# A two-layer transformer trunk on one core: the MLP's first eight blocks by halves of the tokens, and output products without the last pair of heads placed earlier

## The chip, the cores and the metric

One core of one Trainium2 chip runs the whole program. The metric is the device time of one launch in microseconds. A core has TensorE (PE, with its weight loads PEld), VectorE (DVE), ScalarE (ACT), GpSimd (POOL), and SyncE (SP), which issues the DMAs. A number like L238 is a line of the kernel.

## The reference

Two layers over 512 tokens (S) of width 1024 (D). Eight heads are dilated windowed attention, eight are latent attention with low-rank queries and keys.

```python
for l in range(DEPTH):                               # DEPTH = 2
    mod = c_act @ w_mod[l] + b_mod[l]
    sh1, sc1, gt1, sh2, sc2, gt2 = jnp.split(mod, 6, axis=-1)
    h = rms_norm(x, g_norm_mix[l]) * (1.0 + sc1[:, None]) + sh1[:, None]
    proj = h @ w_in[l]
    q_d, k_d, v_d, cq, ckv, k_rope = jnp.split(proj, cuts, axis=-1)
    ...
    o_dil = dilated_attention(q_d, k_d, v_d, positions, slopes)
    o_mla = latent_attention(cq, ckv, k_rope, positions, ...)
    mix = jnp.concatenate([o_dil, o_mla], axis=-1) @ w_out[l]
    x = x + gt1[:, None] * mix
    h = rms_norm(x, g_norm_mlp[l]) * (1.0 + sc2[:, None]) + sh2[:, None]
    y = jnp.square(jax.nn.relu(h @ w_mlp_in[l])) @ w_mlp_out[l]
    x = x + gt2[:, None] * y
```

## The kernel before

Activations lie transposed: x is eight tiles `xT[j]` of 128 features by 512 tokens. Each float32 operand is kept as a high and a low part, and each product is three matmuls into one PSUM bank (`mm3`): high by high (L238), low weight by high (L239), high weight by low (L240). Weights are split as they arrive (`load_split`): SP issues the DMA into a "raw" tile, ACT copies the high part (L233), POOL subtracts it for the low part (L234).

Tiles come from pools by tag, each with a fixed number of buffers. "wh" and "wl" hold split weights, "pt" transposed probabilities, "qk" queries and keys, "ot" outputs of heads, "zz" scratch; in PSUM there are four banks "mm", two "sc" and two "tr". A tile waits until the former user of its buffer is done. A scheduler orders the instructions of each engine when the kernel is built, from the order in which the program issues them; each engine then works through its own list in order.

A layer has these stages.
- Norm and first projection. `norm` works on one half of the tokens: squares and sums (L255 to L259), one matmul for the sum over features (L284), the inverse root on DVE and ACT (L285 to L290), then eight chunks. Even chunks take an "sc" bank (DVE L273, ACT L274, DVE L275), odd ones a "b" tile (DVE L268, ACT L269, POOL L270, L271). High and low parts come out as `h`. In layer 1 the weights of projection 0 (`PR[0]`, 384 columns, four blocks of 128 tokens `tb`) and of the latent projection (`W`, 416 columns) follow each other.
- Heads, two at a time: `heads` yields the steps of a pair, and `weave` puts other work between them at fixed points (the table of numbers; "W1", "OL0" and so on are entries of it). A head ends in ACT L370, DVE L371. The pair then is split: ACT L651 (high), POOL L652 (low), into an "ot" tile. The dilated heads' half of the output projection (`out_dil`) runs during the latent heads.
- The latent heads' half of the output projection. Features j = 0 to 7, each four products k = 0 to 3, where k = 3 is the last pair of heads, for half of the tokens at a time; `add_x` (DVE L659) adds the result to x. In half 0 three features are in flight: products 0 to 2 of j + 1 and j + 2 are issued before product 3 of j.
- The MLP. The first group has eight blocks of 128 features. Blocks 0 to 3 are done for half 0 of the tokens, then for half 1 (24 matmuls of 256 each), blocks 4 to 7 for all tokens (24 matmuls of 512). After each block come the squared relu and its split (ACT L832, DVE L833, ACT L834, DVE L835). Then follow the second MLP product of this group and the other groups. In layer 0, `next_mod` computes the modulation of layer 1 on the side: a DMA into a tile, and DVE L170; two go with each of blocks 4 to 7.

Of the kernel before, what the change touches and what calls it, by code (L numbers as in the profile page):

```python
# [34 lines left out]
    F0=(0, 0), F1=(6.4, 2.33), T0=(3.23, 2.08), T1=(8.8, 8.8), M0=(0, 0), M1=(4, 4), M2=(4.1, 4.1),  # L35
    M3=(6.5, 6.55), LD0=(5, 5), LD1=(9, 9), LM=(6.45, 7.11), LO=(7.2, 7.2), OD0=(3.1, 3.1), OD1=(5.1, 5.1),
    OL0=(3.5, 3.5), OL1=(10.04, 10.04), MV0=(1.5,), MV1=(3.75,), MV2=(5.37,), MV3=(8,), MV4=(0.62,),
    MV5=(6.55,), MP0=(3.45,), MP1=(8.6,), W0=(13.54,), W1=(21.5,), W2=(33,),
)


# [1 line left out]
def trunk(ctx: ExitStack, tc: tile.TileContext, a):  # L43
# [20 lines left out]
    def t4(tag, shape, dt=F32R):  # L64
        return pool.tile(list(shape), dt, tag=tag, bufs=BUFS[tag], name=nm(tag))
# [7 lines left out]
    def ps(tag, shape=(128, 512)):  # L73
        return psum.tile(list(shape), F32, tag=tag, bufs=BUFS[tag], name=nm(tag))
# [138 lines left out]
    def next_mod(**kw):  # L213
        if modq:
            modq.pop(0)(**kw)
# [10 lines left out]
        V.scalar_tensor_tensor(r, t, 1.5, y, op0=OP.add, op1=OP.mult)  # L226
        return r

    def load_split(src, n, raw="raw"):
        raw = t4(raw, [128, 1024], F32)[:, :n]  # L230
        hi, lo = t4("wh", [128, 1024])[:, :n], t4("wl", [128, 1024])[:, :n]
        SY.dma_start(raw, src)
        A.activation(hi, raw, AF.Copy)  # L233
        G.tensor_tensor(lo, raw, f(hi), op=OP.subtract)  # L234
        return hi, lo
# [142 lines left out]
    for l in range(L):  # L378
# [19 lines left out]
        def group(src, n):  # L398
            ws = {}

            def load(i, raw="raw"):
                hi, lo = load_split(src[i], 2 * n, raw)
                ws[i] = (hi.rearrange("p (k n) -> p k n", k=2), lo.rearrange("p (k n) -> p k n", k=2))

            def step(bank, k, tb):
                mm3(bank, hx(hh, k, tb * 128, tb * 128 + 128), hx(hl, k, tb * 128, tb * 128 + 128),
                    ws[k // 2][0][:, k % 2], ws[k // 2][1][:, k % 2], k == 0, k == 7)

            return [lambda i=i, **kw: load(i, **kw) for i in range(4)], step

        def blocks(w, n, step, chain):
            for tb in range(4):
                st = {}

                def mm(k, tb=tb, st=st):
                    if k == 0:
                        st["b"] = ps("mm")
                    step(st["b"][:, :n], k, tb)

                w["mm"].append([lambda k=k, mm=mm: mm(k) for k in range(8)])  # L420
                w["chain"].append(lambda tb=tb, st=st: chain(tb, st["b"]))

        def dil_prep(pr, k_outer=False):
            w = dict(mm=[], chain=[])
            w["load"], step = group(a["win"][l, pr], 384)
            R = {}

            def chain(tb, bank):
                half, t = tb // 2, tb % 2
                if tb == 0:  # L430
                    R["QS"], R["KH"], R["KL"] = (t4("qk", [128, 2, S]) for _ in range(3))
                    R["VD"] = t4("qk", [128, 4, 2, 2, 64])
                if t == 0:
                    R[half] = t4("pt" if k_outer else "zz", [128, 2, 4, 2, 64], F32)

                nb = 2 if l == 0 else 1
                if t == 0 or nb == 1:
                    R["sq"], R["bank"] = s2([128, 4 * nb, 64]), []
                sq, got = R["sq"], R["bank"]
                got.append((t, bank))  # L440
                A.activation(sq[:, 4 * len(got) - 4:4 * len(got)].rearrange("p h d -> p (h d)"), bank[:, 0:256],
                             AF.Square, scale=1.0 / 8)

                def values():
                    src = bank[:, 256:384].rearrange("p (h d) -> p h d", h=2)
                    vt = R["VD"][:, tb]
                    A.activation(vt[:, :, 0], src, AF.Copy)
                    V.tensor_tensor(vt[:, :, 1], src, f(vt[:, :, 0]), op=OP.subtract)

                if nb == 2:  # L450
                    values()
                if len(got) == nb:
                    v = small(4 * nb)
                    V.tensor_reduce(v, sq, axis=AX.X, op=OP.add)
                    rs = rsqrt_tiny(v, 4 * nb, bank)
                    for u, (t_, bk) in enumerate(got):
                        src = bk[:, 0:256].rearrange("p (h o d) -> p h o d", h=4, o=1).to_broadcast([128, 4, 2, 64])
                        scl = rs[:, 4 * u:4 * u + 4].rearrange("p (h o d) -> p h o d", o=1, d=1).to_broadcast([128, 4, 2, 64])
                        V.tensor_tensor(R[half][:, t_], src, scl, op=OP.mult)
                if nb == 1:  # L460
                    values()

            def tail(half):
                dq = R[half]
                for is_k in range(2):
                    tr = ps("mm", (128, 2, 2, 128))
                    for hd in range(2):
                        for t in range(2):
                            T.transpose(tr[:, hd, t], dq[:, t, 2 * is_k + hd].rearrange("p a b -> p (a b)"), ident)  # L469
                    src = tr.rearrange("p h t c -> p h (t c)")  # L470
                    if is_k:
                        kh, kl = R["KH"][:, :, HALF[half]], R["KL"][:, :, HALF[half]]
                        A.activation(kh, src, AF.Copy, scale=kcol)
                        V.scalar_tensor_tensor(kl, src, kcol, f(kh), op0=OP.mult, op1=OP.subtract)
                    else:
                        q = R["QS"][:, :, HALF[half]]
                        A.activation(q, src, AF.Copy)
                        V.tensor_tensor(q[64:128], src[64:128], f(q[64:128]), op=OP.subtract)

            def score(hd, sc, qb):  # L480
                q = R["QS"][:, hd, qb * 128:(qb + 1) * 128]
                T.matmul(sc, q, R["KH"][:, hd], start=True, stop=False)
                T.matmul(sc, q, R["KL"][:, hd], start=False, stop=True)

            w["score"], w["vals"] = score, lambda hd, kc: R["VD"][:, kc, hd].rearrange("p a b -> p (a b)")
            w["tail"] = [lambda half=half: tail(half) for half in range(2)]
            if k_outer:
                w["step"], w["do_chain"] = step, chain
            else:
                blocks(w, 384, step, chain)  # L490
            return w


# [167 lines left out]
        wo = {}  # L661

        def out_load(half, jj):
            hi, lo = load_split(a["wout"][l, half, jj], 1024)
            wo[half, jj] = (hi.rearrange("p (j k m) -> p j k m", j=2, k=4), lo.rearrange("p (j k m) -> p j k m", j=2, k=4))

        def out_dil(j):
# [96 lines left out]
        else:  # L764
            gains()
            for fn in PR[0]["load"]:
                fn()
            run(flow(PR[0], 0, 16) + spread(W["load"], 10, 15.2) + flow(W, 16, 32)
                + [(tn("W0"), PR[0]["tail"][0]), (tn("W1"), PR[0]["tail"][1]), (tn("W2"), W["tail"])])

        for st in range(8):
            ev = []
# [25 lines left out]
            weave(heads(st, PR[st]), ev)  # L798

        h2h, h2l = new_h()  # L800
        for hf in HALF:
            late = []
            for j in range(8):
                wh, wl = wo[1, j // 2]
                p = ps("mm")[:, :256]

                def prod(k, wh=wh, wl=wl, j=j, p=p, hf=hf):
                    mm3(p, wh[:, j % 2, k], wl[:, j % 2, k], OT[4 + k][:, 0, hf], OT[4 + k][:, 1, hf], k == 0, k == 3)

                for k in range(3):  # L810
                    prod(k)

                def finish(prod=prod, j=j, p=p, hf=hf):
                    prod(3)
                    add_x(j, hf, p, gt1)

                late.append(finish)
                if len(late) > (2 if hf.start == 0 and j < 7 else 0):
                    late.pop(0)()
            for fn in late:  # L820
                fn()
            norm(hf, amlp[l], modc[l][:, 24:32], h2h, h2l)


        gt2 = modc[l][:, 40:48]
# [9 lines left out]
            V.tensor_tensor(r2[:, 1, hf], p, f(r2[:, 0, hf]), op=OP.subtract)  # L835

        def w1_tile(i):
            return tuple(t.rearrange("p (k m) -> p k m", k=8) for t in load_split(a["w1"][l, i], 1024))

        R2 = {}  # L840

# [7 lines left out]
        FULL = slice(0, S)  # L849
        for grp in ((0, 8), (8, 16), (16, 24), (24, 28), (28, 32)):  # L850
            rng = range(*grp)
            for i in rng:
                R2[i] = t4(("qk", "ot")[i % 2], [128, 2, S])
            if grp[0] == 0:
                ws = [w1_tile(i) for i in range(4)]
                for hf in HALF:
                    for i in range(4):
                        mlp1(i, hf, ws[i])
                rest = range(4, 8)
            else:  # L860
                rest = rng
            for i in rest:
                mlp1(i, FULL, w1_tile(i))
                if l == 0:
# [91 lines left out]
```

## Time and profile before

| | us |
|---|---|
| median of 3 runs | 1359.0 (1358.58 to 1362.28) |
| profiled execution | 1359.13 |
| its span, first to last instruction | 1357.4 |
| PE busy | 1272.5 |
| mean granted TensorE clock, share of full speed | 0.981 |

The profile lists instructions by line and engine with what ended the idle time before them, as [idle us <-releaser]. The starts of two matmuls in the timeline tell the pace; their listed lengths overlap. In a row of windows the columns are the stretch, its length, the busy time (and number of instructions) of PE, PEld, DVE, ACT and POOL, the granted clock, the DMA's share and GB/s.

### The profile page before, as it was taken

How to read it: one execution, taken by the hardware profiler on the slowest of the kernel's cores; microseconds unless marked ns; L12 is line 12 of the kernel's file. 1: busy time of each engine (PE TensorE's matmuls, PEld its weight loads, DVE VectorE, ACT ScalarE, POOL GpSimd, SP SyncE). 2: the span in 40 equal slices, each digit the busy share in tenths (PEclk: the TensorE clock that was granted, in tenths of full speed). 3: DMA queues.
4: the chain of work that ended last, by engine and by line, in shares of the span. 5: the costliest groups of instructions: out<-in, count | busy, mean ns of one | idle time of the engine just before them, and what ended most of it. 6: DMA issues, size and time to landing. Idle time of an engine off the chain costs nothing.

```text
span 1357.4 us, 19211 instructions
## 1 busy us (share of the span) xinstructions
PE 1272.5 (94%) x6922; PEld 1108.0 (82%) x6922; DVE 752.4 (55%) x1620; ACT 675.5 (50%) x1405; POOL 650.6 (48%) x504
## 2 busy tenths in 40 slices
PE   4878979898899999999998999899889999999999
PEld 2878867787888888888898999798788888888888
DVE  6777797876661661834575577987672122121123
ACT  5567798776541322323245677887654133232321
POOL 5636776671554444444435443444155444444441
PEclk9979998999999999999998999999999999999999
DMA  9325543331254572854532344311013332223221
GB/s 344 111 94 175 177 155 108 104 130 74 63 187 147 189 253 93 280 169 160 170 108 83 90 138 135 94 48 48 1 63 109 96 103 96 93 93 108 95 93 62
DMA packets 57246, 167.59 MB, mean 123 GB/s; under 512 B 8640, under 2 KB 10816, under 8 KB 57152
## 3 DMA queue, kind: packets, MB, share of 16 engines
q1 hardware_dynamic: 57152, 166.38, 37.1%
q8 instruction: 54, 0.88, 0.3%
q14 instruction: 40, 0.33, 0.1%
HBM read 155.87 MB, written 10.49 MB: 123 GB/s over the span
## 4 chain that ended last, share of the span: by engine, by line
PE 72%; DVE 6%; ACT 6%; POOL 4%; issue 4%; DMA 3%; POOLq 0%; ACTq 0%; DVEq 0%
PE mm L238 21%; PE mm L239 21%; PE mm L240 21%; PE tr L368 2%; PE tr L358 2%; POOL wl L234 2%; DMA raw<-in_wout_dram 1%; DVE pt L362 1%; ACT wh L233 1%; DVE P L343 1%; POOL b L339 1%; POOL raw L167 1%; DMA bias<-b 1%; PE sc L238 1%; PE mm L469 1%
## 5 line engine op out<-in xcount | busy, mean ns | idle before, releaser
L234 POOL TENSOR_TENSOR wl<-raw,wh 128x1024 fp32r<-128x1024 f32 (+3 forms) x188 | 425.2, 2266 | 448.9 <-ACT wh L233 426.9
L233 ACT ACTIVATE wh<-raw 128x1024 fp32r<-128x1024 f32 (+3 forms) x188 | 188.8, 1005 | 272.0 <-PE mm L240 206.2
L659 DVE SCALAR_TENSOR_TENSOR x<-mm,mod,x 128x512 f32<-128x512 f32 (+1 forms) x144 | 89.0, 630 | 261.4 <-PE mm L240 261.2
L238 PE MATMUL mm<-h,wh 128*128 128x512 f32 (+1 forms) x608 | 224.5, 370 | 7.1 <-ACT h L274 7.1
L239 PE MATMUL mm<-h,wl 128*128 128x512 f32 (+1 forms) x608 | 224.5, 370 | 0.0
L240 PE MATMUL mm<-h,wh 128*128 128x512 f32 (+1 forms) x608 | 221.8, 369 | 1.1 <-POOL h L271 1.1
L238 PE MATMUL mm<-ot,wh 128*128 128x512 f32 (+1 forms) x448 | 155.9, 350 | 4.5 <-ACT ot L651 4.1
L239 PE MATMUL mm<-ot,wl 128*128 128x512 f32 (+1 forms) x448 | 154.5, 347 | 0.0
L240 PE MATMUL mm<-ot,wh 128*128 128x512 f32 (+1 forms) x448 | 151.4, 348 | 0.2 <-POOL ot L652 0.2
L832 ACT ACTIVATE P<-mm 128x512 f32<-128x512 f32 (+1 forms) x72 | 39.2, 551 | 201.7 <-PE mm L240 201.7
L238 PEld LDWEIGHTS mm<-h,wh 128*128 128x128 f32 x608 | 116.2, 191 | 26.0 <-ACT h L274 7.5
L239 PEld LDWEIGHTS mm<-h,wl 128*128 128x128 f32 x608 | 116.1, 191 | 19.2 <-POOL wl L234 0.2
L240 PEld LDWEIGHTS mm<-h,wh 128*128 128x128 f32 x608 | 114.6, 190 | 20.1 <-POOL h L271 1.5
L833 DVE SCALAR_TENSOR_TENSOR mm<-mm,P 128x512 f32<-128x512 f32 (+1 forms) x72 | 45.4, 636 | 138.9 <-ACT P L832 138.9
L238 PE MATMUL mm<-wh,h 128*128 128x384 f32 (+1 forms) x288 | 98.9, 356 | 15.5 <-ACT h L742 9.8
L239 PE MATMUL mm<-wh,h 128*128 128x384 f32 (+1 forms) x288 | 101.9, 354 | 5.3 <-POOL h L745 3.2
L238 PE MATMUL mm<-qk,wh 128*128 128x512 f32 (+1 forms) x288 | 105.3, 366 | 1.0 <-DVE x L659 1.0
L239 PE MATMUL mm<-qk,wl 128*128 128x512 f32 (+1 forms) x288 | 105.2, 365 | 0.0
L240 PE MATMUL mm<-qk,wh 128*128 128x512 f32 (+1 forms) x288 | 105.2, 365 | 0.0
L355 POOL TENSOR_SCALAR P<-P,hs 128x512 f32<-128x512 f32 x64 | 48.1, 752 | 112.4 <-DVE hs L348 96.7
L240 PE MATMUL mm<-wl,h 128*128 128x384 f32 (+1 forms) x288 | 100.4, 351 | 0.0
L170 DVE SCALAR_TENSOR_TENSOR pt<-pt,cb 128x1024 f32<-128x1024 f32 x56 | 99.1, 1804 | 0.0
(248 smaller groups left out, 2669.0 us busy)
## 6 DMA issues: line engine op xcount, KB each, us to landing
raw<-in_w_dram SPq DMA_DIRECT2D x64, 512.0 KB, 3.3
pt<-in_wmod_dram SPq DMA_DIRECT2D x56, 512.0 KB, 5.0
raw<-in_w2a_dram SPq DMA_DIRECT2D x48, 512.0 KB, 3.5
raw<-in_wmod_dram SPq DMA_DIRECT2D x24, 512.0 KB, 3.6
raw<-in_win_dram SPq DMA_DIRECT2D x30, 384.0 KB, 3.3
bias<-b SPq DMA_DIRECT2D x32, 256.0 KB, 2.0
raw<-in_wout_dram SPq DMA_DIRECT2D x16, 512.0 KB, 3.5
raw<-in_w2b_dram SPq DMA_DIRECT2D x16, 512.0 KB, 3.3
```

The costliest lines, as they stand in the source:

```text
L170: r = V.scalar_tensor_tensor(w, w, 1.0, cb, op0=OP.mult, op1=OP.mult, accum_out=out)
L233: A.activation(hi, raw, AF.Copy)
L234: G.tensor_tensor(lo, raw, f(hi), op=OP.subtract)
L238: T.matmul(out, sh, mh, start=first, stop=False)
L239: T.matmul(out, sl, mh, start=False, stop=False)
L240: T.matmul(out, sh, ml, start=False, stop=last)
L355: G.tensor_scalar(P, P, r_, 0.0, op0=OP.mult, op1=OP.add)
L358: T.transpose(tr[:, kc], P[:, kc * 128:(kc + 1) * 128], ident)
L368: T.matmul(po[:, HALF[qh]], vals(hd, kc), pt[qh][w][:, kc], start=(kc == 0 and w == 0), stop=(kc == 3 and w == 1))
L659: V.scalar_tensor_tensor(xT[j][:, hf], p, gt[:, j:j + 1], xT[j][:, hf], op0=OP.mult, op1=OP.add)
L832: A.activation(r, p, AF.Relu)
L833: V.scalar_tensor_tensor(p, p, 0.0, r, op0=OP.max, op1=OP.mult)
```

## The change

1. `load_split` takes the tags of the buffers for high and low part.
2. MLP, first group: all eight weight tiles are loaded ahead, tiles 0 and 1 into "pt", 2 and 3 into "qk", 4 to 7 into "wh" and "wl", and all eight blocks go by halves. The eight `next_mod` of layer 0 go with half 1.
3. Layer 1's first projections: the latent weights go into "ot" and "pt"; the blocks alternate, `PR[0]` 0 and 1, `W` 0 and 1, then 2 and 3 of each, and `PR[0]` 2 and 3 use "sc" banks. The result of projection 0 lies in "pt" and the second tail comes at 29.5 instead of 21.5 in the table.
4. Output products of the latent half: in half 0, products 0 to 2 of features 4 to 7 are added to x at once, those of features 0 to 3 stay in the four "mm" banks; then product 3 follows for all eight. Weight tile 3 goes into "zz".

```diff
-    MV5=(6.55,), MP0=(3.45,), MP1=(8.6,), W0=(13.54,), W1=(21.5,), W2=(33,),
+    MV5=(6.55,), MP0=(3.45,), MP1=(8.6,), W0=(13.54,), W1=(29.5,), W2=(33,),
...
-    def load_split(src, n, raw="raw"):
+    def load_split(src, n, raw="raw", tags=("wh", "wl")):
...
-                    R[half] = t4("pt" if k_outer else "zz", [128, 2, 4, 2, 64], F32)
+                    R[half] = t4("pt" if pr == 0 else "zz", [128, 2, 4, 2, 64], F32)
...
-                blocks(w, 384, step, chain)
+                blocks(w, 384, step, chain, ("mm", "mm", "sc", "sc") if pr == 0 else ("mm",) * 4)
...
-            hi, lo = load_split(a["wout"][l, half, jj], 1024)
+            hi, lo = load_split(a["wout"][l, half, jj], 1024, tags=("zz", "zz") if half and jj == 3 else ("wh", "wl"))
...
-            run(flow(PR[0], 0, 16) + spread(W["load"], 10, 15.2) + flow(W, 16, 32)
-                + [(tn("W0"), PR[0]["tail"][0]), (tn("W1"), PR[0]["tail"][1]), (tn("W2"), W["tail"])])
+            for i in range(4):
+                W["load"][i](tags=("pt", "pt") if i == 3 else ("ot", "ot"))
+            ev = []
+            for n, (w, tb) in enumerate(((PR[0], 0), (PR[0], 1), (W, 0), (W, 1), (PR[0], 2), (PR[0], 3), (W, 2), (W, 3))):
+                ev += spread(w["mm"][tb], 4 * n, 4 * n + 3.6) + [(4 * n + 3.8, w["chain"][tb])]
+            run(ev + [(tn("W0"), PR[0]["tail"][0]), (tn("W1"), PR[0]["tail"][1]), (tn("W2"), W["tail"])])
...
-        for hf in HALF:
-            late = []
-            for j in range(8):
...
+        def out_lat(j, p, hf, ks, first, last):
+            wh, wl = wo[1, j // 2]
+            for k in ks:
+                mm3(p, wh[:, j % 2, k], wl[:, j % 2, k], OT[4 + k][:, 0, hf], OT[4 + k][:, 1, hf],
+                    first and k == ks[0], last and k == ks[-1])
+        hf, held = HALF[0], {}
+        for j in (4, 5, 6, 7, 0, 1, 2, 3):
+            p = ps("mm")[:, :256]
+            out_lat(j, p, hf, (0, 1, 2), True, j >= 4)
+            if j >= 4:
+                add_x(j, hf, p, gt1)
+            else:
+                held[j] = p
+        for j in range(8):
+            p = held[j] if j < 4 else ps("mm")[:, :256]
+            out_lat(j, p, hf, (3,), j >= 4, True)
+            add_x(j, hf, p, gt1)
+        norm(hf, amlp[l], modc[l][:, 24:32], h2h, h2l)
...
+            tags = ("wh", "wl") if i >= 4 else ("pt", "pt") if i < 2 else ("qk", "qk")
...
+            ws = [w1_tile(i) for i in range(8)] if grp[0] == 0 else []
...
-                ws = [w1_tile(i) for i in range(4)]
                 for hf in HALF:
-                    for i in range(4):
+                    for i in range(8):
                         mlp1(i, hf, ws[i])
-                rest = range(4, 8)
+                        if l == 0 and hf.start and i:
+                            next_mod(tag="pt", pin=True)
+                            if i == 7:
+                                next_mod(tag="pt", pin=True)
+                rest = ()
```

What the scheduler makes of it shows in each engine's list. TensorE at the MLP's first group of layer 0, where half 0 ends and half 1 begins: before, with `h_3876` the first tile of normalized input and `wh_4263` the weights of block 0, the list has the following.

```order
L238 MATMUL mm_4376<-h_3882,wh_4281 128x256
L239 MATMUL mm_4376<-h_3882,wl_4282 128x256
L240 MATMUL mm_4376<-h_3883,wh_4281 128x256
L238 MATMUL mm_4406<-h_3876,wh_4263 128x256
L239 MATMUL mm_4406<-h_3876,wl_4264 128x256
```

That is block 3 of half 0 followed at once by block 0 of half 1. After, at the same place:

```order
L238 MATMUL mm_4408<-h_3882,qk_4281 128x256
L239 MATMUL mm_4408<-h_3882,qk_4282 128x256
L240 MATMUL mm_4408<-h_3883,qk_4281 128x256
L238 MATMUL mm_4438<-h_3876,wh_4287 128x256
L239 MATMUL mm_4438<-h_3876,wl_4288 128x256
```

Block 3 of half 0 is followed by block 4 of half 0 (`wh_4287`); blocks 4 to 7 are 96 matmuls, and the first of half 1 (on `pt_4263`) comes behind them.

POOL at the last pair of heads of layer 0 (`P_` are probabilities, `ot_3867` the last pair's tile, `raw_` weights as loaded), before:

```order
L355 TENSOR_SCALAR P_3811<-P_3811,hs_3810 128x512
L355 TENSOR_SCALAR P_3836<-P_3836,hs_3835 128x512
L652 TENSOR_TENSOR ot_3867<-o_3622,ot_3867 128x512
L234 TENSOR_TENSOR wl_4264<-raw_4262,wh_4263 128x1024
L234 TENSOR_TENSOR wl_4270<-raw_4268,wh_4269 128x1024
```

and after:

```order
L355 TENSOR_SCALAR P_3811<-P_3811,hs_3810 128x512
L234 TENSOR_TENSOR qk_4282<-raw_4280,qk_4281 128x1024
L355 TENSOR_SCALAR P_3836<-P_3836,hs_3835 128x512
L234 TENSOR_TENSOR wl_4288<-raw_4286,wh_4287 128x1024
L234 TENSOR_TENSOR pt_4264<-raw_4262,pt_4263 128x1024
L234 TENSOR_TENSOR pt_4270<-raw_4268,pt_4269 128x1024
L652 TENSOR_TENSOR ot_3867<-o_3622,ot_3867 128x512
```

Four splits of the MLP's weights, of tiles 3, 4, 0 and 1, now stand ahead of the last pair's L652, where they stood behind it or much later.

ACT at the same place, before:

```order
L361 ACTIVATE pt_3744<-tr_3816 128x4x128
L361 ACTIVATE pt_3744<-tr_3841 128x4x128
L370 ACTIVATE o_3622<-tr_3848 64x512
L651 ACTIVATE ot_3867<-o_3622 128x512
L255 ACTIVATE sc_3998<-x_77 128x256
```

and after:

```order
L361 ACTIVATE pt_3744<-tr_3816 128x4x128
L233 ACTIVATE wh_4287<-raw_4286 128x1024
L361 ACTIVATE pt_3744<-tr_3841 128x4x128
L233 ACTIVATE pt_4263<-raw_4262 128x1024
L233 ACTIVATE pt_4269<-raw_4268 128x1024
L370 ACTIVATE o_3622<-tr_3848 64x512
L651 ACTIVATE ot_3867<-o_3622 128x512
```

Three high parts now stand ahead of the last head's L370; the last two write buffers that its own products read (pt).

More of the change, by code (lines that the diff above doesn't have):

```diff
@@ L227, in rsqrt_tiny @@
         return r
-    def load_split(src, n, raw="raw"):
+    def load_split(src, n, raw="raw", tags=("wh", "wl")):
         raw = t4(raw, [128, 1024], F32)[:, :n]
-        hi, lo = t4("wh", [128, 1024])[:, :n], t4("wl", [128, 1024])[:, :n]
+        hi, lo = t4(tags[0], [128, 1024])[:, :n], t4(tags[1], [128, 1024])[:, :n]
         SY.dma_start(raw, src)
@@ L399, in group, with load @@
             ws = {}
-            def load(i, raw="raw"):
-                hi, lo = load_split(src[i], 2 * n, raw)
+            def load(i, raw="raw", tags=("wh", "wl")):
+                hi, lo = load_split(src[i], 2 * n, raw, tags)
                 ws[i] = (hi.rearrange("p (k n) -> p k n", k=2), lo.rearrange("p (k n) -> p k n", k=2))
@@ L409, in group, with blocks @@
             return [lambda i=i, **kw: load(i, **kw) for i in range(4)], step
-        def blocks(w, n, step, chain):
+        def blocks(w, n, step, chain, tags=("mm",) * 4):
             for tb in range(4):
@@ L416, in mm @@
                     if k == 0:
-                        st["b"] = ps("mm")
+                        st["b"] = ps(tags[tb])
                     step(st["b"][:, :n], k, tb)
@@ L800, in trunk @@
         h2h, h2l = new_h()
-        for hf in HALF:
-            late = []
-            for j in range(8):
[L804 to L822, printed above, removed]
+        def out_lat(j, p, hf, ks, first, last):
[16 more added lines that the diff above has]
+        norm(hf, amlp[l], modc[l][:, 24:32], h2h, h2l)
+        hf = HALF[1]
+        for j in range(8):
+            p = ps("mm")[:, :256]
+            out_lat(j, p, hf, (0, 1, 2, 3), True, True)
+            add_x(j, hf, p, gt1)
+        norm(hf, amlp[l], modc[l][:, 24:32], h2h, h2l)
         gt2 = modc[l][:, 40:48]
@@ L837, in w1_tile @@
         def w1_tile(i):
-            return tuple(t.rearrange("p (k m) -> p k m", k=8) for t in load_split(a["w1"][l, i], 1024))
+            tags = ("wh", "wl") if i >= 4 else ("pt", "pt") if i < 2 else ("qk", "qk")
+            return tuple(t.rearrange("p (k m) -> p k m", k=8) for t in load_split(a["w1"][l, i], 1024, tags=tags))
         R2 = {}
@@ L851, in trunk @@
             rng = range(*grp)
+            ws = [w1_tile(i) for i in range(8)] if grp[0] == 0 else []
             for i in rng:
                 R2[i] = t4(("qk", "ot")[i % 2], [128, 2, S])
+            rest = rng
             if grp[0] == 0:
-                ws = [w1_tile(i) for i in range(4)]
                 for hf in HALF:
-                    for i in range(4):
+                    for i in range(8):
                         mlp1(i, hf, ws[i])
-                rest = range(4, 8)
-            else:
-                rest = rng
+                        if l == 0 and hf.start and i:
[3 more added lines that the diff above has]
+                rest = ()
             for i in rest:
```

## The prediction

> **What bounds the kernel now.** I read the page first, then the waits of PE, then the timeline and windows at the waits that the change touches. The page says who the bound is.
>
> ```profile
> PE 1272.5 (94%) x6922; PEld 1108.0 (82%) x6922; DVE 752.4 (55%) x1620; ACT 675.5 (50%) x1405; POOL 650.6 (48%) x504
> PE 72%; DVE 6%; ACT 6%; POOL 4%; issue 4%; DMA 3%; POOLq 0%; ACTq 0%; DVEq 0%
> PE mm L238 <- ACT h L274: 10.8, 3, 3.7
> PE mm L238 <- ACT ot L651: 4.1, 2, 2.1
> ```
>
> TensorE is busy for 1272.5 of 1357.4 us. All it does is needed, so time is to be had only from its idle 85 us, from its half-speed stretches, and from shape (narrow matmuls cost more per column). Two rows of waits are the change's targets: three waits for the first normalized tile (L274), 10.8 us together, and two for the last pair of heads (L651), 4.1 us. The timeline places them, and the windows show what a wait costs beyond itself.
>
> ```profile
> 361.48 0.59 PE L284 MATMUL tr<-P,ones 128*128 128x256 f32 x2
> 367.46 0.47 ACT L274 ACTIVATE h<-sc,mod 128x256 fp32r<-128x256 f32 x1 [1.86 <-DVE sc L273]
> 367.99 0.58 PE L238 MATMUL mm<-h,wh 128*128 128x256 f32 x1 [3.53 <-ACT h L274]
> 1013.03 0.58 PE L238 MATMUL mm<-h,wh 128*128 128x256 f32 x1 [3.53 <-ACT h L274]
> 1013.42 0.42 PE L239 MATMUL mm<-h,wl 128*128 128x256 f32 x1
> 1013.63 0.41 PE L238 MATMUL mm<-h,wh 128*128 128x256 f32 x1
> ...
> 368.00:370.50 2.50, 2.50 (x11) 2.50 (x12) 2.27 (x7) 1.86 (x5) 1.82 (x3) 0.50 0.00 0
> 370.50:372.00 1.50, 1.50 (x11) 1.50 (x11) 1.35 (x4) 1.10 (x3) 1.40 (x3) 0.75 0.06 11
> ...
> 1007.07 0.28 PE L240 MATMUL mm<-h,wh 128*128 128x256 f32 x1
> 1007.19 0.28 PE L238 MATMUL mm<-h,wh 128*128 128x256 f32 x1
> 1060.00:1290.00 230.00, 230.00 (x1017) 190.50 (x1016) 44.10 (x62) 64.71 (x83) 101.42 (x43) 1.00 0.30 99
> ```
>
> Windows run: length, busy time of PE, PEld, DVE, ACT, POOL, then the granted clock. After the 3.53 us wait the clock is 0.50 for 2.5 us and 0.75 on average over the next 1.5, so half speed lasts about 3.25 us; the starts there are 0.213 us apart (1013.42 to 1013.63) instead of 0.12 (1007.07 to 1007.19): some 14 matmuls at 0.093 extra, 1.3 us. The last row prices the full-width form: 1017 matmuls in 230 us, 0.226 each.
>
> **Part 1, the MLP by halves (both layers).** Before, half 0 of the tokens has 4 blocks of 24 matmuls of 256; the sums for half 1 (L284) go through PE at 361.48, the first h of half 1 starts at 367.46, and PE waits from 364.46. After, 8 blocks stand there. In the order, 12 + 96 matmuls come between the last L284 and the first matmul of half 1: 108 x 0.12 = 13.0 us, against the 6.0 + 0.5 us that the chain from L284 to the first h takes (361.48 to 367.93). The wait goes, and with it the half clock: -3.53 - 1.3. The cost: blocks 4 to 7 are cut from 96 matmuls of 512 to 192 of 256: 96 x (2 x 0.12 - 0.226) = +1.3. Net -3.5 per layer, -7.0 for both. What is late next is nothing on this chain: 6.5 us of slack remain, which also covers an L284 that runs a few us later. By the Trainium skill ("TensorE: Matmul & The Clock Gate", section on the back-to-back issue gap) a warm matmul starts every N/2.4 ns + 2.5 ns, an estimate of 109.2 ns at 256 and 215.8 at 512. By that the narrow form would cost 96 x 2.5 ns = 0.24 us per layer instead of 1.3, and the part would bring 2.1 us more; this trace's spacings, 0.12 and 0.226, are longer than both, and I keep them.
>
> Covers in this part. A block's PSUM bank comes back through L832, L833 and L835.
>
> ```profile
> 362.89 0.64 ACT L832 ACTIVATE P<-mm 128x256 f32<-128x256 f32 x2
> 364.29 0.42 DVE L835 TENSOR_TENSOR qk<-mm,qk 128x256 fp32r<-128x256 f32 x1
> L170 DVE SCALAR_TENSOR_TENSOR pt<-pt,cb 128x1024 f32<-128x1024 f32 x56 | 99.1, 1804 | 0.0
> pt<-in_wmod_dram SPq DMA_DIRECT2D x56, 512.0 KB, 5.0
> ```
>
> That takes 1.8 us (362.89 to 364.71); block 4 starts 22 matmuls (2.6 us) after block 0's last, so I cost it at nothing (1 us per layer if ACT is late). In layer 0 all eight steps of the next layer's modulation move into half 1: 8 x 1.8 = 14.4 us of DVE beside 8 blocks' own work, in 192 x 0.12 = 23 us. The tiles that they load into stand in the buffers of weight tiles 0 and 1, free only after blocks 0 and 1 of half 1 (2.9 and 5.8 us in), and a load takes 5.0 us. DVE may stand still for the first of them, with posts of blocks behind it; four banks give PE about three blocks (8.6 us) of cover. Cost zero, up to 4.
>
> **Part 2, output products of the last pair (both layers).** Before, 36 of the 96 matmuls of half 0 run ahead of the last pair's result; after, 72. So 36 x 0.12 = 4.3 us leave the path behind it.
>
> ```profile
> 328.47 0.59 ACT L370 ACTIVATE o<-tr 64x512 f32<-64x512 f32 x1 [1.91 <-PE tr L368]
> 329.81 0.63 ACT L651 ACTIVATE ot<-o 128x512 fp32r<-128x512 f32 x1 [0.75 <-DVE o L371]
> 330.49 0.58 PE L238 MATMUL mm<-ot,wh 128*128 128x256 f32 x1 [2.06 <-ACT ot L651]
> 330.52 1.27 POOL L652 TENSOR_TENSOR ot<-o,ot 128x512 fp32r<-128x512 f32 x1 [5.82 <-ACT ot L651]
> 332.82 0.48 DVE L659 SCALAR_TENSOR_TENSOR x<-mm,mod,x 128x256 f32<-128x256 f32 x1 [3.04 <-PE mm L240]
> 975.49 0.58 PE L238 MATMUL mm<-ot,wh 128*128 128x256 f32 x1 [2.06 <-ACT ot L651]
> ...
> 300.00:331.00 31.00, 24.59 (x156) 19.95 (x155) 21.03 (x41) 22.55 (x48) 9.54 (x10) 0.99 0.21 75
> 331.25:334.00 2.75, 2.75 (x15) 2.52 (x14) 1.18 (x3) 0.60 (x2) 0.54 (x1) 0.55 0.90 347
> 925.00:976.00 51.00, 45.45 (x290) 38.64 (x288) 33.45 (x66) 36.87 (x76) 14.69 (x18) 0.99 0.06 22
> ...
> L234 POOL TENSOR_TENSOR wl<-raw,wh 128x1024 fp32r<-128x1024 f32 x144 | 344.3, 2394 | 386.2 <-ACT wh L233 381.3 <-PE mm L240 2.7 <-PE mm L239 1.5
> L233 ACT ACTIVATE wh<-raw 128x1024 fp32r<-128x1024 f32 x144 | 152.3, 1057 | 257.6 <-PE mm L240 202.2 <-issue 46.0 <-DMA raw<-in_wout_dram 5.6
> ```
>
> They cost nothing only where PE was idle. PE's idle time before the last pair is 6.4 us in layer 0 (31.00 - 24.59) and 5.5 in layer 1, of each 2.06 the wait at the end, which stays (it is the chain L370, L371, L651). In layer 0 28 of them stand in one row ahead of the last head's score, that is on the chain that ends in L651: 28 x 0.12 = 3.4 us later. In layer 1 they are spread (9 ahead of a score, 11 ahead of transposes, 16 among the last products), with 2.8 us of delay by my count. Second, the first two tiles of w1 now take the score buffers (pt): in ACT's order one split (L233, 1.06 us) comes between the last products and L370 or L651, and in POOL's order the low part (L234, 2.39 us) comes ahead of L652. So the high part of the last pair comes 3.4 + 1.06 = 4.4 us later in layer 0 and 3.8 in layer 1. The low part comes 1.06 + 2.39 + 1.27 = 4.7 us after the products end, instead of 1.97 + 1.27 + 0.1 = 3.3. PE can bridge from the high part (3.0 us after the products) with 8 matmuls at the half clock (0.55 in 331.25:334.00, so this seam has it already), 1.7 us, to 4.7 us: just enough in layer 0; in layer 1 POOL is 0.6 us later by its queue. With four more additions on DVE (L659, 0.48 each, one of them behind the last bank): layer 0 -4.3 + 4.4 + 0.3 + 0.4 = +0.8, layer 1 -4.3 + 3.8 + 0.6 + 0.9 = +1.0. Bounds: all gaps filled and no split in the way, -4 each; PE held until a whole second L234 has gone too, +3 each. I take the middle, +1.8, because the rows of ACT and POOL stand where they stand and these engines work in order. By the Trainium skill ("GPSIMD Engine Reference", section on elementwise cycle accounting) Pool needs about 2.6 cycles of 1.2 GHz per element of a row, an estimate of 2.2 us for 1024; by that the low part would come 0.2 us earlier. The trace has 2.39, and that is used.
>
> **Part 3, the layer seam.** Half 1's first projection waited for h, and PE then ran slowly.
>
> ```profile
> 719.15 0.59 PE L284 MATMUL tr<-P,ones 128*128 128x256 f32 x2
> 724.14 1.01 PE L238 MATMUL mm<-wh,h 128*128 128x384 f32 x2 [3.71 <-ACT h L274]
> 725.72 0.69 PE L239 MATMUL mm<-wh,h 128*128 128x384 f32 x1 [0.57 <-DVE h L275]
> 729.08 0.52 PE L240 MATMUL mm<-wl,h 128*128 128x384 f32 x1
> 729.40 0.46 PE L238 MATMUL mm<-wh,h 128*128 128x384 f32 x1
> 729.88 0.34 PE L240 MATMUL mm<-wl,h 128*128 128x384 f32 x1
> 730.05 0.33 PE L238 MATMUL mm<-wh,h 128*128 128x384 f32 x1
> 756.46 0.35 PE L239 MATMUL mm<-wh,h 128*128 128x416 f32 x1
> 756.65 0.35 PE L240 MATMUL mm<-wl,h 128*128 128x416 f32 x1
> ```
>
> At 0.32 (729.08 to 729.40) against 0.17 us per matmul, the half clock to 729.5 costs 2 us beside the waits of 3.71 and 0.57: 6.2 in all. After, 48 latent matmuls of half 0 (48 x 0.19 = 9.1 us) stand ahead. Against that: the splits of the latent weights (four L234) now stand among POOL's norm steps, so I put L284 of half 1 at about 722.8 instead of 719.15; the two products of half 1 use "sc" banks, which the norm's own sums hold until L275 of the fifth and seventh chunk, by an estimate 3.7 us after the first h: 722.8 + 5.0 (719.15 to 724.10, as before) + 3.7 puts their first matmul at 731.5. Before, the same amount of work was done at 724.14 + 9.1 = 733.2: 1.7 gained, and about 1 of the half clock. The normalization of the query and key of half 1 then ends the stage with less work behind it: I charge 2.5. Net 0, between -4 (the 6.2 less the tail) and +4 (tail and banks in full). The order of the first heads of layer 1 differs too; +-2, counted at 0.
>
> **The sum.** -7.0 + 1.8 + 0 = -5.2 on the profiled 1359.13 (span 1357.4), which lies on the median 1359.0: 1354.
>
> **Rivals.** A, the moved matmuls fall into idle time: part 2 brings 3.5 per layer, part 3 brings 4: 1359 - 7 - 7 - 4 = 1341, with only one of the two about 1347. For it speak the 6.4 and 5.5 us of idle; against it that PE is at work for 45.45 of 51 us and that 28 matmuls stand in one row. B, slower: POOL's order. L652 stands behind splits whose tiles must first be loaded, converted and given the last heads' buffers. If PE must wait for the low part until two full L234 have gone after the last products, each layer loses 4.8 + 1.27 - 1.7 = 4.4 beyond the +4.4 of the chain, less the 4.3: +4.5 per layer; with 3 to 5 of the tail at the seam the MLP's 7 are used up and the time is 1364 to 1366. It decides from a wait of 4 us for the low part on. Against it: the first of the two tiles can be split while the last products run. C, the wait changes place: part 1's gain stands, but DVE's modulation steps in layer 0 (up to 4) and parts 2 and 3 (+2 to +3 together beyond my sum) eat it: 1357 to 1362.
>
> **How the numbers follow.** Forecast (1350 to 1357) 0.50; A (1340 to 1350) 0.17; C 0.20; B 0.13. A measurement of this kernel can tell about 0.3%, 4.1 us: faster means under 1354.9. The whole of A and three quarters of the forecast's case lie there, 0.54; the rest and C make no difference, 0.33; B 0.13. For 8 in 10 the range takes the forecast, C, and the near half of A: 1345 to 1362.5.
>
> **What would show it.** Right: no wait on h L274 at the second half of the MLP's first blocks, clock 1.00 there in both layers; eight blocks of 24 narrow matmuls per half, 23 us each; L651 of the last pair some 4 us later than 329.81, with L233 on pt just ahead of it, and L652 behind an L234; at the seam the L284 of half 1 near 723. Wrong: waits of PE for posts (L835) or banks in half 1; a wait for ot's low part over 4 us; or a last pair that comes no later than before, which would be rival A.

## The result, and the profile after

The changed kernel takes 1353.45 us (median of 5 runs, 1350.98 to 1354.11) against 1358.99: a ratio of 0.9945, 95% interval 0.9929 to 0.9961. The forecast was 1354.0. The sum came out by luck: its terms did not, and most of what follows is about that.

The page of the profiled execution after (1351.23 us, span 1349.5), first the busy times, then the chain that ended last and PE's two waits for the last pair of heads:

```profile
span 1349.5 us, 19637 instructions
PE 1271.8 (94%) x7114; PEld 1116.2 (83%) x7114; DVE 761.6 (56%) x1644; ACT 680.4 (50%) x1421; POOL 653.0 (48%) x504
PE 66%; POOL 2%; DVE 2%; ACT 2%; issue 2%; DMA 1%; POOLq 0%; DVEq 0%; ACTq 0%
PE mm L238 <- ACT ot L651: 5.2, 2, 2.9
PE mm L240 <- POOL ot L652: 2.2, 2, 1.8
```

The row of 10.8 us for h (L274) is gone from PE's list; the wait for the last pair has grown from 4.1 to 5.2, and one for its low part, 2.2, is new. To see where the time went I split both traces at the same events: L651 of the sixth and of the first pair of heads, the first matmul of the MLP, the first of its second product, and L284 of the seam. The entries are differences to before, worked out from the starts of these instructions; the last row ends with the start of the last matmul.

```
stage                       before   after
start to pair 6, layer 0    295.12   -2.32
pair 6 to MLP, layer 0       56.17   +5.40
MLP, first group             51.53   -4.28
rest of the MLP             299.85   +0.03
L284 of the seam to pair 1  102.78   -7.10
pair 1 to pair 6, layer 1   137.54   +1.11
pair 6 to MLP, layer 1       53.36   +3.55
MLP, first group             51.55   -4.30
rest of the MLP             305.79   +0.03
sum                        1353.69   -7.88
```

The first row is no work of the change: up to there TensorE's list holds the same work in the same order, but for 8 output products (1 us) that come later after, and the entries of this kind differ by -2.9 to +2.2 us between the profiled executions below. Without it the change is -5.6 us, which is what the medians show. An entry under 1 us says little: in the two kernels below that have only the layer seam changed, and layer 0 as before, the second row is +0.40 and +0.88.

The MLP's seam in layer 0, from the timeline after and from a window over half 1 of the eight blocks, from its first matmul to the first of the second product:

```profile
378.46 0.28 PE L240 MATMUL mm<-h,wh 128*128 128x256 f32 x1
378.58 0.28 PE L238 MATMUL mm<-h,pt 128*128 128x256 f32 x1
378.70 0.28 PE L239 MATMUL mm<-h,pt 128*128 128x256 f32 x1
378.58:401.62 23.04, 23.04 (x195) 23.04 (x194) 14.81 (x25) 8.92 (x19) 6.56 (x3) 1.00 0.59 195
```

Half 1 begins at 378.58 without a wait, at the full clock, and its 192 matmuls take 23.04 us, 0.12 each (the window counts three more that overlap its edges).

The last pair of layer 0 and of layer 1, where before PE started at 330.49 and 975.49:

```profile
329.37 1.06 ACT L233 ACTIVATE wh<-raw 128x1024 fp32r<-128x1024 f32 x1 [1.48 <-DMA raw<-in_w_dram]
330.33 0.58 ACT L361 ACTIVATE pt<-tr 128x512 fp32r<-128x512 f32 x1
332.82 4.68 POOL L234 TENSOR_TENSOR pt<-raw,pt 128x1024 fp32r<-128x1024 f32 x2
333.22 1.06 ACT L233 ACTIVATE pt<-raw 128x1024 fp32r<-128x1024 f32 x1 [1.36 <-PE tr L368]
334.30 0.59 ACT L370 ACTIVATE o<-tr 64x512 f32<-64x512 f32 x1
336.32 0.58 PE L238 MATMUL mm<-ot,wh 128*128 128x256 f32 x1 [2.93 <-ACT ot L651]
337.44 1.29 POOL L652 TENSOR_TENSOR ot<-o,ot 128x512 fp32r<-128x512 f32 x1
338.79 1.22 PE L240 MATMUL mm<-ot,wh 128*128 128x256 f32 x4 [0.39 <-POOL ot L652]
973.41 0.44 PE L238 MATMUL mm<-ot,wh 128*128 128x256 f32 x1 [2.29 <-ACT ot L651]
977.18 1.22 PE L240 MATMUL mm<-ot,wh 128*128 128x256 f32 x4 [1.83 <-POOL ot L652]
```

A split that belongs to the MLP's fifth weight tile waits 1.48 us on ACT for its DMA, with the last head's L361 behind it; another sits between the last products and L370; on POOL L652 ends a queue of two splits.

The seam, where before the first product of half 1 waited 3.71 us and then ran at 0.50:

```profile
720.59 0.59 PE L284 MATMUL tr<-P,ones 128*128 128x256 f32 x2
728.20 0.46 PE L238 MATMUL sc<-wh,h 128*128 128x384 f32 x1 [0.46 <-DVE h L275]
724.00:728.00 4.00, 3.75 (x21) 3.38 (x19) 4.00 (x11) 3.39 (x9) 2.31 (x4) 1.00 0.34 98
728.00:732.00 4.00, 3.80 (x22) 3.80 (x23) 3.52 (x13) 3.19 (x15) 2.84 (x5) 1.00 0.20 66
```

The wait is 0.46 us and the clock stays at 1.00.

### The profile page after: what moved, and what is told of

Same layout as the page of the kernel before. It is cut to its first block, busy times and chain, and to the rows that moved or that the text cites. A ratio compares the mean times of both kernels' runs of the same rounds, so it can differ in the third digit from the quotient of the medians.

```text
span 1349.5 us, 19637 instructions
## 1 busy us (share of the span) xinstructions
PE 1271.8 (94%) x7114; PEld 1116.2 (83%) x7114; DVE 761.6 (56%) x1644; ACT 680.4 (50%) x1421; POOL 653.0 (48%) x504
## 4 chain that ended last, share of the span: by engine, by line
PE 66%; POOL 2%; DVE 2%; ACT 2%; issue 2%; DMA 1%; POOLq 0%; DVEq 0%; ACTq 0%
PE mm L240 20%; PE mm L238 20%; PE mm L239 20%; PE tr L368 2%; PE tr L358 1%; POOL wl L234 1%; PE sc L238 1%; PE sc L239 1%; PE sc L240 1%; POOL pt L234 1%; PE sc L482 0%; PE mm L469 0%; DVE pt L362 0%; PE sc L483 0%; PE mm L626 0%
## 5 line engine op out<-in xcount | busy, mean ns | idle before, releaser
L234 POOL TENSOR_TENSOR wl<-raw,wh 128x1024 fp32r<-128x1024 f32 (+3 forms) x174 | 395.7, 2276 | 440.1 <-ACT wh L233 436.4
L233 ACT ACTIVATE wh<-raw 128x1024 fp32r<-128x1024 f32 (+3 forms) x174 | 174.6, 1004 | 263.9 <-PE mm L240 211.7
L238 PE MATMUL mm<-h,wh 128*128 128x512 f32 (+1 forms) x544 | 198.5, 365 | 0.2
L239 PE MATMUL mm<-h,wl 128*128 128x512 f32 (+1 forms) x544 | 198.1, 364 | 0.0
L240 PE MATMUL mm<-h,wh 128*128 128x512 f32 (+1 forms) x544 | 197.9, 364 | 0.0
L238 PE MATMUL mm<-ot,wh 128*128 128x512 f32 (+1 forms) x416 | 147.9, 357 | 7.3 <-ACT ot L651 5.2
L239 PE MATMUL mm<-ot,wl 128*128 128x512 f32 (+1 forms) x416 | 146.7, 354 | 0.0
L240 PE MATMUL mm<-ot,wh 128*128 128x512 f32 (+1 forms) x416 | 144.2, 354 | 2.2 <-POOL ot L652 2.2
L238 PEld LDWEIGHTS mm<-h,wh 128*128 128x128 f32 x544 | 102.6, 189 | 16.8 <-DVE qk L846 0.6
L239 PEld LDWEIGHTS mm<-h,wl 128*128 128x128 f32 x544 | 102.7, 189 | 16.1
L240 PEld LDWEIGHTS mm<-h,wh 128*128 128x128 f32 x544 | 102.6, 189 | 16.2
L239 PE MATMUL mm<-qk,wl 128*128 128x512 f32 (+1 forms) x288 | 105.3, 365 | 0.0
L355 POOL TENSOR_SCALAR P<-P,hs 128x512 f32<-128x512 f32 x64 | 48.4, 756 | 106.0 <-DVE hs L348 85.2
L362 DVE TENSOR_TENSOR pt<-tr,pt 128x512 fp32r<-128x512 f32 x128 | 86.6, 683 | 19.1 <-ACT pt L361 18.5
L238 PEld LDWEIGHTS mm<-ot,wh 128*128 128x128 f32 x416 | 80.1, 193 | 19.2 <-ACT ot L651 5.7
L238 PE MATMUL mm<-wh,h 128*128 128x384 f32 x240 | 81.0, 352 | 11.8 <-ACT h L742 9.8
```

Source lines behind the costliest of these rows:

```text
L238: T.matmul(out, sh, mh, start=first, stop=False)
L239: T.matmul(out, sl, mh, start=False, stop=False)
L240: T.matmul(out, sh, ml, start=False, stop=last)
L355: G.tensor_scalar(P, P, r_, 0.0, op0=OP.mult, op1=OP.add)
L362: V.tensor_tensor(lo, tr, f(hi), op=OP.subtract)
```

## The experiments

**The three parts alone, and the change without its output products.** Each takes its hunks of the diff shown above into the kernel before; the fourth takes the output products' hunks out of the changed kernel.

```diff
# e1: MLP alone
+                    for i in range(8):
+                        mlp1(i, hf, ws[i])
...
# e2: output products alone
+        for j in (4, 5, 6, 7, 0, 1, 2, 3):
...
# e3: layer seam alone
+                blocks(w, 384, step, chain, ("mm", "mm", "sc", "sc") if pr == 0 else ("mm",) * 4)
...
# e4: changed kernel without the output products
-        for j in (4, 5, 6, 7, 0, 1, 2, 3):
+        for hf in HALF:
+            late = []
...
```

> The kernel before with the MLP part alone (eight blocks by halves, weight tiles ahead in pt and qk, the eight modulation steps with half 1). Both theories: the MLP's first group itself gives about 4.3 us per layer (351.29 to 402.82 before, 354.37 to 401.62 after), 8.6 in all. Theory S (the loss at the last pair of heads comes from the weight splits that stand ahead of L370, L651 and L652): 2 to 3 us per layer are lost there again, 1355. Theory M (the loss there comes from the moved output products on the chain): at most 1 us per layer is lost, 1351 to 1352.

> The kernel before with the output products' part alone; no split of MLP weights stands ahead of the last pair's L652 in POOL's order here. Theory S: the 36 moved matmuls are worth 2 to 4 us per layer, 1352 to 1355. Theory M: they stand on the chain of the last pair and cost as much as they save or more, 1359 to 1363.

> The kernel before with the layer seam's part alone. By the two traces the first pair of layer 1 ends 7.1 us earlier against the seam's start, and 1.1 us of it are lost by the sixth pair: 6 us, 1353. Rival: that gain needs the MLP's part (the order of layer 1 shifts with it), or is given back in layer 1's heads: 1357 to 1359.

> The changed kernel with the output products as before (MLP part and layer seam kept). Theory S: the splits still stand ahead of the last pair, so 2 to 3 us per layer are lost there: 1359 - 8.6 - 6 + 5 = 1349 to 1350. Theory M: without the moved products the loss at the last pair falls to at most 1 us per layer: 1345 to 1346.

Measured, against 1359.05 of before: the MLP alone 1364.42 (ratio 1.0035, interval 1.0023 to 1.0048), the output products alone 1360.36 (1.0006, 0.9995 to 1.0017), the seam alone (e3) 1352.22 (0.9945, 0.9932 to 0.9958), MLP and seam 1357.42 (0.9983, 0.9972 to 0.9994). The differences to before by stage:

```
stage                       MLP alone  products alone  seam alone  MLP + seam
pair 6 to MLP, layer 0        +4.30        +0.68         +0.40       +6.29
MLP, first group              -3.53        +0.71         -0.08       -3.51
L284 of the seam to pair 1    +0.88        +0.46         -7.09       -7.16
pair 1 to pair 6, layer 1     +1.00        +0.42         +0.31       +1.17
pair 6 to MLP, layer 1        +5.52        +1.18         -0.75       +6.38
MLP, first group              -3.54        -0.76         +0.03       -3.54
```

Theory S was right in its sign and far too small, also for MLP and seam (1349 to 1350 expected): by itself the MLP part makes the kernel slower, since what its halves bring (7.1 us) is lost again ahead of it (9.8 us), between the sixth pair of heads and the MLP, in code that it doesn't touch. Theory M holds for the output products alone, which bring nothing, but it had them as the cause of the loss at the last pair, and the MLP alone has that loss without them. Beside the splits they are even worth 4 us: MLP and seam take 1357.42, the whole change 1353.45. The seam alone is worth as much as the whole change.

The MLP's first group brings 3.5 us per layer here, not the 4.3 that both theories expected. In the MLP alone and in MLP and seam, PE waits in half 0, in both layers, for the squared relu of an earlier block; in the changed kernel the longest wait in the group is 0.15.

```profile
369.25 0.39 PE L238 MATMUL mm<-h,wh 128*128 128x256 f32 x1 [0.66 <-DVE qk L835]
```

**The splits behind the last pair.** Now the order in ACT's and POOL's queue alone is changed: the splits of some w1 tiles are queued behind L651 and L652 of the last pair, with no wait added. Three tiles first, in the changed kernel, in MLP and seam, and in the MLP alone; and by itself L652 of the last pair on DVE.

```diff
+            last[:] = [getattr(q, "ins", q) for q in (
+                A.activation(ot[:, 0], o, AF.Copy),
+                G.tensor_tensor(ot[:, 1], o, f(ot[:, 0]), op=OP.subtract))]
...
+            with ExitStack() as es:
+                if i in (0, 1, 4):
+                    for q in last:
+                        es.enter_context(tc.issue_after(q))
+                return tuple(t.rearrange("p (k m) -> p k m", k=8) for t in load_split(a["w1"][l, i], 1024, tags=tags))
...
# f3: changed kernel, L652 of the last pair on DVE
-            G.tensor_tensor(ot[:, 1], o, f(ot[:, 0]), op=OP.subtract)
+            (V if st == 7 else G).tensor_tensor(ot[:, 1], o, f(ot[:, 0]), op=OP.subtract)
```

> The changed kernel, with the splits of w1 tiles 0, 1 and 4 queued behind the last pair's L651 on ACT and L652 on POOL (an order in the queue, no wait). Theory S2 (these splits in front of the last pair are the loss, and POOL and ACT have room for them behind it): between the sixth pair and the MLP's start the change loses 5.4 and 3.6 us against before; what remains without the splits is what the output products alone lose, 0.7 and 1.2. So 7 us come back: 1346 to 1347. Rival N: the norm of half 0 then ends last (as it does with the output products alone, where PE waits 1.94 us for h in front of the MLP of layer 1), or the splits behind the last pair delay the norm's steps on ACT and POOL: 2 to 4 us come back, 1349 to 1351.

> MLP part and layer seam, the output products as before, the splits of w1 tiles 0, 1 and 4 behind the last pair. Against the same kernel without that order (1357.4) the 6.3 and 6.4 us between the sixth pair and the MLP's start come back by S2: 1345. By rival N some of it stays lost: 1348 to 1351.

> The changed kernel with L652 of the last pair on DVE instead of POOL; the splits on ACT stay ahead of it. PE's waits for the low part, 0.39 and 1.83 us, go; half clock makes it a little more: 1350 to 1351 by S2, of which this is only the POOL part. If POOL's queue were the whole loss (S1): 1346.

> The MLP part alone with the splits behind the last pair. S2: the 4.3 and 5.5 us lost there come back from 1364.4: 1354 to 1355. If the MLP part loses because eight tiles ahead crowd SP's queue, the raw buffers and POOL whatever their order, it stays at 1360 or more.

Measured, against 1359.61: all parts (f1) 1349.12 (0.9919, 0.9903 to 0.9935), MLP and seam (f2) 1350.33 (0.9928, 0.9913 to 0.9943), low part on DVE (f3) 1351.89 (0.9934, 0.9916 to 0.9951), MLP alone (f4) 1356.62 (0.9983, 0.9972 to 0.9994). So the splits' place was the loss, for the larger part: the MLP alone turns from slower to faster by 7.8 us, and the stretches from the sixth pair to the MLP fall from +4.30 and +5.52 to +1.61 and +1.67. POOL's queue alone (the low part on DVE) is the smaller share at most: 1351.89 against 1353.45 of the changed kernel, with intervals that overlap. But neither f1 nor f2 gave all that S2 expected, nor did the MLP alone (1354 to 1355), and the traces of f1 and f2 show two reasons. In f2 pairs 7 and 8 of layer 1 still took 34.59 us instead of 31.82, and POOL's timeline shows why:

```profile
954.91 0.70 POOL L355 TENSOR_SCALAR P<-P,hs 128x512 f32<-128x512 f32 x1 [0.79 <-DVE hs L348]
957.88 2.36 POOL L234 TENSOR_TENSOR qk<-raw,qk 128x1024 fp32r<-128x1024 f32 x1 [2.27 <-PE sc L239]
960.23 0.69 POOL L355 TENSOR_SCALAR P<-P,hs 128x512 f32<-128x512 f32 x1
```

The split of tile 3 waits 2.27 us for a buffer that the last scores read (sc L239), and the last head's L355, whose input was there at 956.6, starts behind it at 960.23. In f1 the norm of half 0 comes last, rival N in part:

```profile
988.82 0.39 PE L238 MATMUL mm<-h,pt 128*128 128x256 f32 x1 [1.95 <-ACT h L274]
```

**All five tiles behind the last pair**, without and with the output products.

```diff
-                if i in (0, 1, 4):
+                if i in (0, 1, 2, 3, 4):
```

> MLP part and layer seam, output products as before, the splits of w1 tiles 0 to 4 all behind the last pair's L651 and L652. With only tiles 0, 1 and 4 there, the sixth to the eighth pair still took 1.25 and 2.8 us longer than before, with L234 of tile 3 on POOL between the L355 of the last head. If that split is the rest of the loss, 4 us come back: 1346. Rival: tiles 2 and 3 then find POOL or ACT busy with the norm (five L233 of 1.06 us ahead of or between the squares), and the MLP's start comes later by as much: 1350 or more.

> The whole change with the splits of w1 tiles 0 to 4 behind the last pair. The moved output products then cost the last two pairs what they save later (in the kernel with tiles 0, 1, 4 held, the sixth to eighth pair took 4.1 and 4.2 us longer than before and the rest 2.0 and 1.8 less), so no better than the same kernel with the output products as before: 1347 to 1349. If the splits of tiles 2 and 3 were what made the pairs longer here, and the moved products run in idle time: 1344 to 1345.

Measured, against 1359.22: without the products (g1) 1346.14 (0.9896, 0.9877 to 0.9915), with them (g2) 1351.48 (0.9936, 0.9913 to 0.9959). The first came out as expected; the second missed both of its ranges (1347 to 1349, 1344 to 1345). The first is the fastest of all; it beats the changed kernel by about 7 us. Its timeline at the last pair of layer 1:

```profile
964.04 0.39 PE L238 MATMUL mm<-ot,wh 128*128 128x256 f32 x1 [2.06 <-ACT ot L654]
964.07 1.29 POOL L655 TENSOR_TENSOR ot<-o,ot 128x512 fp32r<-128x512 f32 x1 [8.66 <-ACT ot L654]
965.32 2.41 POOL L234 TENSOR_TENSOR pt<-raw,pt 128x1024 fp32r<-128x1024 f32 x1
967.67 2.42 POOL L234 TENSOR_TENSOR qk<-raw,qk 128x1024 fp32r<-128x1024 f32 x1
```

The low part (L655 in this kernel) comes right after the high part (L654), and the splits follow; POOL had stood idle for 8.66 us. Pairs 7 and 8 of layer 1 take 31.81 us, as before (31.82), and the stretches from the sixth pair to the MLP are +0.67 and -0.75. The -0.75 is no gain of the order: the seam alone, which has this stretch as before, shows it too, and in both the half clock behind the last pair's wait is missing (last section).

The two kernels differ only in the output products, so they price these cleanly. From the sixth to the eighth pair it is 39.35 with and 36.02 without in layer 0, 35.21 and 31.81 in layer 1: 3.3 and 3.4 us of the 36 x 0.12 = 4.3 stand on the chain of the last pairs. From there to the MLP it is 17.85 and 20.82, 20.24 and 20.80: only 3.0 and 0.6 come back (in layer 1 without the products there was no half clock, which is worth 0.7 of the difference), and the MLP's first group is 1.1 and 0.5 us longer with them. PE has 122 instead of 158 matmuls between the last pair and the MLP, and now waits for the norm:

```profile
990.81 0.38 PE L238 MATMUL mm<-h,pt 128*128 128x256 f32 x1 [2.72 <-ACT h L274]
```

**What the seam's gain hangs on.** The seam alone (h1), with projection 0 in the four mm banks as before.

```diff
-                blocks(w, 384, step, chain, ("mm", "mm", "sc", "sc") if pr == 0 else ("mm",) * 4)
+                blocks(w, 384, step, chain)
```

> The layer seam alone (as in the run that gave 1352.2), but with projection 0's blocks 2 and 3 in mm banks instead of sc banks. The prediction let the sc banks delay those products by 2.1 us; the trace of the changed kernel shows a wait of 0.46 for them. If the sc banks are what lets them start in time, four mm banks (two of them under the latent products of half 0) come free later and part of the 7 us is lost: 1354 to 1356. If the order of the blocks alone brings the gain, 1352.

Measured 1358.86 against 1359.75 (0.9995, 0.9984 to 1.0006): the whole gain is gone, more than either expectation allowed; the stretch from L284 to the first pair is -0.36 instead of -7.09. PE meets this ahead of the products of half 1:

```profile
735.36 0.33 PE L469 MATMUL mm<-ident,pt 128*128 128x128 f32 x1 [3.31 <-DVE st L226]
```

It is the transpose of projection 0's first half, which now stands ahead of the products that need its banks, and waits 3.31 us for the inverse roots (L226). The products of half 1 begin only at 738.26, 32.4 us after the seam's first L284, instead of 26.7 in the changed kernel (728.20 less 701.50). With the sc banks they run ahead of that transpose.

## Why the prediction was right, and where its terms were not

The time, 1353.45, is close to 1354.0 by luck, since three wrong terms cancel. By the traces:

- **Part 1, -7.0 forecast, -8.6 measured** (-4.28 and -4.30). The mechanism stood: the wait went, no modulation step or bank held PE for more than 0.08 us, DVE was busy for 14.81 of the 23.04 us of half 1. The half clock had cost 1.5 rather than 1.3 (the 96 matmuls of half 1 before took 13.04 us, 367.99 to 381.03, not 11.5), and a wait of 0.56 us for the low part of h at the start of the stage fell to 0.15. By itself the part brought the 7.1 that its sum says; the wait for a block's bank, which the prediction put at nothing, was 0.66 us per layer there, and it is gone beside the moved products. The trace's 0.12 us per narrow matmul held. By the estimate of 109 ns from the Trainium skill ("TensorE: Matmul & The Clock Gate", section on the back-to-back issue gap) this part would have brought 2.1 us more; the trace does not agree with it.
- **Part 2, +1.8 forecast, +8.95 measured** (+5.40 and +3.55), outside its bounds of -8 to +6. L651 of the last pair came 8.1 and 5.1 us later after the sixth pair than before, not some 4. What was right: the 36 matmuls stand on the chain, L233 sits between the last products and L370, L652 behind two L234. What failed is the count of what stands ahead of the last pair. The prediction priced the splits of tiles 0 and 1 and passed over the other rows that the orders ahead of it show: L233 of tile 4, which waits 1.48 us for its DMA with L361 behind it, and L234 of tile 3 between the two L355. A split was priced by its length (1.06, 2.39), not by the time at which its input or its buffer is there. Putting them behind the last pair gave back 5.6 and 7.1 us in the kernel with MLP and seam (+6.29 and +6.38 became +0.67 and -0.75, 0.7 of the latter by the clock). I also forecast the norm as harmless; f1 and g2 show it as the next wait, 1.95 and 2.72 us.
- **Part 3, 0 forecast, -7.1 measured**, outside its bounds of -4 to +4. Three sub-steps failed, all to the dark side. The banks of the norm delayed the products by 0.46 us and L284 came 2.6 us later against the seam's start instead of 3.65, so they began 2.1 us earlier than I had them; the half clock went altogether (2 us, of which I had counted 1) with the 0.57 us wait beside it; and the 2.5 us charged for the normalization at the end did not occur: the waits of L482 there are 0.23 and 0.56 us, against 0.54 and 0.44 for L482 and L537 before. For that charge the prediction had no row at all. These come to about 6.2 of the 7.1 us; the rest is not followed. And I had the sc banks as a cost; h1 shows them as the condition of the gain.
- **Rivals.** A's seam came true, its output products did the opposite. B's mechanism was there (PE waited 1.83 us for the low part in layer 1), below the 4 us from which it was to decide. C named the wrong places: the modulation steps took nothing in the MLP, and parts 2 and 3, which were to lose 2 to 3 us together beyond the sum, cancel, with 7 lost by one and 7 won by the other.

In layer 1, 1.0 to 1.8 us are lost, more than the 0 that the prediction counted for the order of the first heads, between the first and the sixth pair in every kernel with the MLP part, and 0.3 to 0.5 in the others. Most of it, 0.8 to 1.5, lies between the second and the third pair. There DVE waits for the load of a bias tile, 1.13 us in the changed kernel and 1.2 to 1.8 in all others with the MLP part except the MLP alone, where the wait is 1.08 and its releaser is POOL; before, DVE had no such wait there.

```profile
851.55 0.69 DVE L343 CUSTOM_DVE_ANT_0 P<-sc,b 128x512 f32<-128x512 f32 x1 [1.13 <-DMA b<-bias]
```

Why that load lands later stays open. The 0.67 us that g1 loses ahead of the MLP of layer 0 lies between the +0.40 and +0.88 that the seam alone and h1 show there with layer 0 as before.

## What to carry to other kernels

Work that is loaded ahead is only free if each engine's list has it behind what the critical chain needs: an instruction that is ready late, or whose buffer is, holds all that stands behind it in that engine's order (in f2 the split of tile 3 kept the last head's L355 waiting for 3.7 us, with 2.36 us of work of its own), so price it by when it can start and not by its length. Moving matmuls ahead of a late input pays only while PE is idle for that input: the same 36 were worth 4 us where the splits made the last pair late, nothing by themselves, and cost 5 us once all five splits stood behind it. What then ends last (here the norm) sets the next limit. Run the parts of a change alone: here one of three (the seam) brings alone as much as all of it, another cost more than it brought until five splits were put behind the last pair, and with that order and without the third the kernel is 7 us faster than with the whole change.

## What the runs showed of the hardware

Whether a wait of PE halves its clock does not follow from the length of the wait alone. In layer 1 of the changed kernel, behind waits of 2.29 and 1.83 us, PE was still at 0.50 from 977 to 980; before, the half clock at the 2.06 us wait lasted 3.4 us (330.30 to 333.70). In layer 0 of the changed kernel the clock was down already ahead of the 2.93 us wait, from 331.90 on, and still at 341, so its 0.50 is not the doing of that wait and the 0.39 us behind it alone. The windows' columns are as in the prediction; the rows are of the changed kernel, then of before, the seam alone (e3) and g1.

```profile
330.50:331.90 1.40, 0.59 (x2) 0.40 (x3) 0.69 (x1) 1.35 (x2) 1.40 (x1) 1.00 0.00 0
331.90:336.30 4.40, 1.49 (x7) 1.20 (x6) 0.68 (x1) 2.28 (x3) 4.40 (x3) 0.50 0.41 127
336.30:339.00 2.70, 2.29 (x9) 2.00 (x10) 0.00 (x0) 0.00 (x0) 2.43 (x2) 0.50 0.68 222
339.00:341.00 2.00, 2.00 (x9) 1.77 (x10) 1.59 (x5) 1.07 (x3) 0.00 (x0) 0.50 0.52 209
977.00:980.00 3.00, 2.82 (x12) 2.60 (x13) 2.20 (x6) 1.37 (x4) 0.12 (x1) 0.50 0.44 162
...
330.30:333.70 3.40, 3.21 (x13) 2.98 (x14) 0.88 (x3) 0.44 (x2) 1.27 (x1) 0.50 0.94 367
...
331.20:334.60 3.40, 3.01 (x20) 2.61 (x21) 1.59 (x5) 1.02 (x3) 1.28 (x1) 1.00 0.98 400
...
964.00:967.40 3.40, 2.98 (x20) 2.58 (x21) 1.56 (x4) 3.40 (x6) 3.33 (x2) 1.00 0.02 5
```

The last two rows stand behind the same wait of 2.06 us, and there the clock stayed at 1.00. PE had been as busy ahead of it: 4.02 of 6 us before (322 to 328) and 4.01 in the seam alone (322.72 to 328.72), which has the same instructions there. So neither the wait nor the share of busy time ahead of it decides; what does is open. The half clock is worth 0.7 us here: from the last pair to the MLP it is 21.5 us before and 20.8 in the seam alone, in both layers.

The Trainium skill ("TensorE: Matmul & The Clock Gate", the part on the clock gate) lets the clock fall after an idle window of about 3.4 us that runs freely. The 2.06 us wait of before already halved it, so the trace does not agree with 3.4 us as a bound on a single wait.
